# Modulation vectors on VectorE, norms read from PSUM, split weights at block 2's entry: one change to a two-block transformer kernel

## The chip, the cores and the metric

The kernel runs on one core of one Trainium2 chip. The metric is the device time of one execution in microseconds, and lower is better. A core has five engines that matter here: TensorE (PE, matmuls), VectorE (DVE), ScalarE (ACT), GpSimd (POOL) and SyncE (SP), which issues most transfers. Each engine takes its instructions in the order of its own queue, and semaphores order the engines among each other. SBUF is the memory on the chip, PSUM the eight banks (2 KB a partition each) into which TensorE writes.

## What is computed

256 tokens of width 1024 go through two blocks. The first is a mixer of three branches, a cross attention and 32 experts; the second has two layers, each with a mixer, a feed-forward part, and modulation by vectors that come from a condition `c`. Cut to what matters here:

```python
a = a_in[..., :D] * sigmoid(a_in[..., D:])
a = silu(layer_norm(causal_depthwise_conv(a, conv_a_w) + conv_a_b))
y_a = a @ w_a_out + b_a_out
y_b = (gate_b * causal_depthwise_conv(gate_c * v_bc, conv_b_w)) @ w_b_out
y_c = einsum(multiscale_pool(pool_in), pool_w) * pool_scale    # windows 2, 4, 8, 16
m = sigmoid(g_a) * y_a + sigmoid(g_b) * y_b + sigmoid(g_c) * y_c
x = layer_norm(ALPHA * x + m @ w_mix_out)
x = layer_norm(ALPHA * x + cross_attention(x, layer_norm(mem)))
x = layer_norm(ALPHA * x + experts(x))                         # top 4 of 32
for layer in range(2):                                         # block 2
    shift_m, scale_m, gate_m, shift_f, scale_f, gate_f = split(silu(c) @ ada_w[layer] + ada_b[layer], 6)
    h = rms_norm(x) * (1 + scale_m) + shift_m
    x = x + gate_m * (attention(h) if layer == 0 else retention(h))
    h = rms_norm(x) * (1 + scale_f) + shift_f
    x = x + gate_f * swiglu(h)
```

All is in float32.

## The kernel before, in words

Activations lie with features on the 128 partitions, in eight chunks of 128 features by 256 tokens. A **product** (`product`, L407) makes two chunks of output from eight chunks of input: 48 matmuls of 128x256, three for each pair, since each operand is split in a high and a low half. The halves of a weight are made on the chip by `Weights.split` (L276 to L293): ScalarE copies the high half `wh` (L289), VectorE subtracts it for the low half `wl` (L290), two splits of 128x1024 a product. GpSimd does the subtraction where the running number of the split stands in `ASIDE`. Raw weights come in tiles of 2 MB from a ring of five (`RB`), which the modulation tiles `wadb` share; all these loads go out on SP's queue. Activations are split the same way by `split` (L475 on ScalarE, L476 on VectorE).

The program is one long sequence of products. Two hooks put other work among them: `spare[0]()` is called as each product starts, and `pump` runs queued background steps (the 31 taps of the convolution, the chunks of a norm) at points within it. A scheduler then orders each engine's queue, so the order of emission is what the code decides.

**Block 1** runs the products `a1`, `a2`, four of pooling, then twelve of the short convolution (`gate_c`, `v_bc`, `gate_b` for each of four groups `j`), `pool_w`, the gate of the third branch, eight of gate and `yb`, four of `ga`, four of keys, four of values, four of `ya`, four of the mixing output, then cross attention, router and experts. A pooling product's result is written by ScalarE to `up`, one part of the tile `pads` (L756); GpSimd forms the window sums from it in one to four steps (L762). All four groups use the same pads.

**Norms** are made by `Stat`: squares and sums per chunk, TensorE sums over features (`sums`, L495 being one of the matmuls of `spread`), `roots` forms mean and reciprocal root, and `spread` (L488 to L496) writes a vector of tokens across the partitions of a PSUM tile by two matmuls with a diagonal made on VectorE (L494) or ScalarE (L492). `normal` then does, per chunk, the addition of the mean (L571), the multiplication by gain and root (L574), and a split. The mean is copied from PSUM to SBUF (`tmp_mu`) by ScalarE ahead of L571, and every third L571 is on GpSimd.

**Modulation vectors**: `vector_ada` (L608 to L628) handles 24 tiles `wadb` of four blocks, 128x1024 each, 96 blocks in all. A block is multiplied by `silu(c)` spread over the partitions (`cb`) and summed. By `POOLED`, 60 blocks are multiplied on GpSimd (L621) and summed on ScalarE (L622); the other 36 are one instruction on VectorE (L624). L626 adds the bias after each fourth block. A tile's load is issued when its first block is due. In block 1, 24 blocks run from the value products on (`early`: two a product in the first four, then one); after the experts `later` runs as many as `DUE` says, one a product from the fourth call on. `silu_c` (L605) computes `silu(c)` on ScalarE, which needs another table of functions.

**Entry of block 2.** The last norm of block 1 and the first of block 2 are done at once: `scale3` spreads four vectors to PSUM (`nmc`, `rrc`, `rmc`, `rsc`), `h0` makes each chunk of the input for block 2 (L1288 add, L1290 ScalarE, L1291, L1293 add, then `split` to `HH`, `HL`), and `back` restores the chunk of the running sum. Four products run first on uncorrected input, and `fix3` corrects their results (L1271, L1273, L1275, and L1276 on GpSimd).

Of the kernel before, what the change touches and what calls it, by code (L numbers as in the profile page):

```python
# [11 lines left out]
F32 = mybir.dt.float32  # L12
# [17 lines left out]
F3 = 1  # L30
# [17 lines left out]
DUE = '0001111111111111111'  # L48
# [5 lines left out]
POOLED = (4, 2)  # L54
TWO = 4
UB3 = 4
K3 = 4
GA = (1, 3, 5, 7)
GB = ()
ASIDE = (3, 5, 7, 9)  # L60
# [49 lines left out]
def host_layout(inp):  # L110
# [204 lines left out]
def program(ctx: ExitStack, tc: tile.TileContext, A, out, stop=None):  # L315
# [182 lines left out]
    class Stat:  # L498
# [23 lines left out]
        def finish(self, eps):  # L522
            self.sums()
            self.roots(eps)
            return self.nm
# [13 lines left out]
        def roots(self, eps):  # L539
# [3 lines left out]
            if self.center:  # L543
# [12 lines left out]
            b = psum([128, T], tag="st", bufs=2)  # L556
# [6 lines left out]
    def normal(src, dst, H, L, c, nm, g, b, func=None):  # L563
# [32 lines left out]
    vec = [None, 0, 0]  # L596
    cbs = []
    where = [0]

    def silu_c(pool, after=None):  # L600
# [3 lines left out]
        with paced() if after is None else behind(after):  # L604
            i = S.activation(cb, cb, AF.Silu).ins  # L605
        cbs[:] = [cb]
        return i

    def vector_ada(n=1):

        for _ in range(n):
            if vec[0] is None:
                if not late:
                    return
                vec[:] = [B.raw.tile([128, 4, D], F32, tag="raw", name="wadb"), 0, late.popleft()]
                nc.sync.dma_start(vec[0], A["wadb"][vec[2]])
# [42 lines left out]
    def router_constants():  # L659
# [5 lines left out]
        G.memset(rwx[:, :, NE:], 1.0 / D)  # L665
        for k in range(NCH):
# [1247 lines left out]
```

## Time and profile before

| | |
|---|---|
| time of three runs, us | 2196.34, 2203.99, 2202.17; median 2202.17 |
| the profiled execution, us | 2199.12 |
| its span in the profile, us | 2197.2 |
| TensorE busy | 2090.4 us, 95% |
| VectorE, ScalarE, GpSimd busy | 53%, 36%, 24% |
| mean clock granted to TensorE | 0.975 of full speed |

The span runs from the first to the last instruction in the trace; the profiled execution's own time has 1.9 us around it. The busy shares are means over stages with different limits: the experts, from some 460 to 1400 us, wait for transfers, the rest is paced by TensorE and by what feeds it. The page is read for where to look, the table by stretch for which stretch loses time, and the waits and the groups of such a stretch for what it loses it to.

### The profile page before, as it was taken

The page shows a single profiled execution, that of the slowest core. Times are in us where ns is not written, and L with a number is a line of the kernel's source. Part 1 is how long each engine was busy: PE and PEld are TensorE (multiplying, and loading weights), DVE is VectorE, ACT ScalarE, POOL GpSimd, SP SyncE. Part 2 cuts the span into 40 slices and gives each one's busy share as a digit, 9 for nine tenths or more (in the row PEclk, how much of TensorE's full clock was granted, in tenths as well). Part 3 has the DMA queues.
Part 4 walks back from the last instruction along what each step waited for, and adds up shares of the span by engine and source line. Part 5 has one row for each costly group of instructions (what it writes and reads, how often), then busy time and mean ns, then how long its engine had stood idle before and what let it go on. Part 6 is the DMA issues. An engine that isn't in the chain of part 4 may idle for free.

```text
span 2197.2 us, 32992 instructions
## 1 busy us (share of the span) xinstructions
PE 2090.4 (95%) x13668; PEld 1522.4 (69%) x13668; DVE 1159.1 (53%) x1815; ACT 800.1 (36%) x1374; POOL 532.7 (24%) x444
## 2 busy tenths in 40 slices
PE   8999988999998999999999999979999999999998
PEld 8999988873443333333333333568899999999998
DVE  6798888832322222222211112388797678877553
ACT  5576665630000000000000000365575465546443
POOL 2648386412000000000000000176412123310000
PEclk9999989999999999999999999989999999999999
DMA  8445555689999999999999999844377567555440
GB/s 347 165 158 192 200 202 197 246 330 394 392 420 384 428 428 427 426 428 427 428 427 427 427 427 428 352 155 159 124 301 274 209 237 272 227 191 225 189 154 20
DMA packets 49595, 650.57 MB, mean 296 GB/s; under 512 B 5632, under 2 KB 7552, under 8 KB 10656
## 3 DMA queue, kind: packets, MB, share of 16 engines
q1 hardware_dynamic: 48096, 645.45, 72.2%
q10 hardware_dynamic: 1344, 2.95, 0.4%
q8 instruction: 109, 1.79, 0.3%
q14 instruction: 46, 0.38, 0.0%
HBM read 647.33 MB, written 1.05 MB: 295 GB/s over the span
## 4 chain that ended last, share of the span: by engine, by line
PE 51%; DMA 5%; DVE 5%; issue 3%; ACT 2%; POOL 1%; DVEq 0%; ACTq 0%; POOLq 0%
PE ps_mm L1720 9%; PE ps_mm L418 8%; PE ps_mm L420 8%; PE ps_mm L419 8%; PE ps_st L1883 7%; DMA wgu<-in_wgu 5%; PE ps_tp L1774 2%; PE ps_tp L1707 1%; PE ps_mm L443 1%; PE ps_mm L444 1%; DVE act L1760 1%; PE ps_mm L445 1%; DVE wl L290 1%; POOL tmp_pd L1759 1%; PE ps_mm L1636 1%
## 5 line engine op out<-in xcount | busy, mean ns | idle before, releaser
L290 DVE TENSOR_TENSOR wl<-wraw,wh 128x1024 fp32r<-128x1024 f32 x352 | 487.4, 1387 | 192.7 <-ACT wh L289 190.5
L289 ACT ACTIVATE wh<-wraw 128x1024 fp32r<-128x1024 f32 x356 | 375.3, 1056 | 266.7 <-PE ps_mm L419 238.4
L1720 PE MATMUL ps_mm<-wgu,xs 128*64 128x512 f32 x2048 | 454.6, 594 | 7.5 <-DMA wgu<-in_wgu 6.9
L1720 PEld LDWEIGHTS ps_mm<-wgu,xs 128*64 128x64 f32 x2048 | 145.6, 137 | 287.7 <-issue 270.9
L1883 PE MATMUL ps_st<-wdn,actT 128*64 128x512 f32 x1024 | 233.3, 602 | 5.6 <-DVE actT L1768 5.6
L418 PE MATMUL ps_mm<-HH,wh 128*128 128x256 f32 x832 | 235.8, 284 | 0.7 <-ACT wh L289 0.7
L420 PE MATMUL ps_mm<-HH,wl 128*128 128x256 f32 x832 | 234.4, 284 | 1.7 <-DVE wl L290 1.7
L419 PE MATMUL ps_mm<-HL,wh 128*128 128x256 f32 x832 | 235.7, 284 | 0.0
L1756 DVE TENSOR_SCALAR tmp_pd<-ps_mm 128x512 f32<-128x512 f32 x32 | 22.1, 692 | 381.7 <-PE ps_mm L1720 381.6
L1759 POOL TENSOR_TENSOR tmp_pd<-tmp_pd,tmp_stat 128x512 f32<-128x512 f32 x32 | 40.1, 1275 | 752.9 <-ACT tmp_stat L1757 752.9
L621 POOL TENSOR_TENSOR wadb<-wadb,cb 128x1024 f32<-128x1024 f32 x60 | 169.4, 2848 | 141.7 <-DMA wadb<-in_wadb 101.6
L418 PE MATMUL ps_mm<-pairA,wh 128*128 128x256 f32 x640 | 184.1, 290 | 12.6 <-ACT wh L289 7.8
L1757 ACT ACTIVATE tmp_stat<-tmp_pd 128x512 f32<-128x512 f32 x32 | 20.1, 631 | 469.1 <-DVE tmp_pd L1756 469.1
L419 PE MATMUL ps_mm<-pairA,wh 128*128 128x256 f32 x640 | 184.0, 288 | 1.9 <-DVE pairA L476 1.9
L420 PE MATMUL ps_mm<-pairA,wl 128*128 128x256 f32 x640 | 181.7, 287 | 1.3 <-DVE wl L290 1.3
L1883 PEld LDWEIGHTS ps_st<-wdn,actT 128*64 128x64 f32 x1024 | 73.8, 138 | 139.5 <-issue 129.1
L420 PEld LDWEIGHTS ps_mm<-HH,wl 128*128 128x128 f32 x832 | 158.7, 192 | 3.0 <-DVE wl L290 2.3
L418 PEld LDWEIGHTS ps_mm<-HH,wh 128*128 128x128 f32 x832 | 159.4, 192 | 1.8 <-ACT wh L289 1.2
L419 PEld LDWEIGHTS ps_mm<-HL,wh 128*128 128x128 f32 x832 | 159.6, 192 | 0.9 <-issue 0.7
L418 PEld LDWEIGHTS ps_mm<-pairA,wh 128*128 128x128 f32 x640 | 125.6, 197 | 13.8 <-ACT wh L289 7.8
L419 PEld LDWEIGHTS ps_mm<-pairA,wh 128*128 128x128 f32 x640 | 126.0, 197 | 2.3 <-DVE pairA L476 2.3
L420 PEld LDWEIGHTS ps_mm<-pairA,wl 128*128 128x128 f32 x640 | 124.8, 196 | 1.7 <-DVE wl L290 1.7
(460 smaller groups left out, 4176.3 us busy)
## 6 DMA issues: line engine op xcount, KB each, us to landing
wgu<-in_wgu SPq DMA_DIRECT2D x128, 2048.0 KB, 22.5
wdn<-in_wdn SPq DMA_DIRECT2D x62, 2048.0 KB, 19.8
wraw<-in_wpost SPq DMA_DIRECT2D x56, 2048.0 KB, 7.7
wraw<-in_wpre SPq DMA_DIRECT2D x32, 2048.0 KB, 7.8
wadb<-in_wadb SPq DMA_DIRECT2D x24, 2048.0 KB, 9.1
wdn<-in_wdn SPq DMA_DIRECT2D x8, 512.0 KB, 24.4
wraw<-in_wpre SPq DMA_DIRECT2D x4, 512.0 KB, 8.0
wraw<-in_wpost SPq DMA_DIRECT2D x4, 512.0 KB, 11.7
```

The lines of the kernel that those rows point to most:

```text
L289: self.ins = (nc.scalar.activation(wh, src, AF.Copy).ins, (eng or nc.vector).tensor_tensor(wl, src, wh.bitcast(F32), op=ALU.subtract).ins)
L290: (eng or nc.vector).tensor_tensor(wl, src, wh.bitcast(F32), op=ALU.subtract).ins)
L418: PE.matmul(pts[m], wh[:, w], XH[:, kc, :width], start=(i == 0), stop=False)
L419: PE.matmul(pts[m], wh[:, w], XL[:, kc, :width], start=False, stop=False)
L420: PE.matmul(pts[m], wl[:, w], XH[:, kc, :width], start=False, stop=(i == n - 1))
L443: PE.matmul(pts[t], XH[:, kc, x], wh, start=(i == 0), stop=False)
L621: G.tensor_tensor(w[:, i, :], w[:, i, :], cbs[0], op=ALU.mult)
L1720: i_ = PE.matmul(banks[j][row[x]], xs[:, k, row[x]], r["g", k][:, x, 512 * j:512 * j + 512], start=False, stop=(k == NCH - 1))
L1756: V.tensor_scalar(g, banks[h], 7.0, None, op0=ALU.min)
L1759: G.tensor_tensor(g, g, s, op=ALU.mult)
L1774: PE.matmul(p[:, m, :], Y[:, (2 * c + m) * 128:(2 * c + m) * 128 + 128], GST, start=True, stop=True)
L1883: PE.matmul(yb[j][row[x]], actT[:, k, row[x]], r["d", j, k // 4][:, k % 4, x, :], start=(k == 0), stop=(k == NCH - 1))
```

## The change

1. **Modulation vectors.** All 96 blocks run as one VectorE instruction each. A tile's load is issued when the third block of the tile before has been emitted (`ada_load`, `coming`). The 24 blocks of block 1 start at the gate and `yb` products, and `EARLY` says how many each product gets: one in each of gate, `yb` and `ga`, none with keys and values, two with `ya`, one with the mixing output. After the experts `DUE` gives none in the first six calls and two in calls 17 to 19. `silu_c` runs ahead of the gate products; block 2's SiLU moves from the entry to the call with number 5.
2. **Norms.** With `bank=True` (memory norm, convolution norm, the rms norms of block 2) the mean's spread is made by ScalarE and stays in PSUM, in one bank with the root's; all L571 are on VectorE, and intermediate results lie in PSUM too.
3. **Entry of block 2.** The four spread vectors lie in two banks, `h0` is all VectorE with `nmc` and `w` in PSUM, `fix3` uses GpSimd every other time, and ten splits in place of four have their low half made on GpSimd.
4. **Pooling** product `j` is followed by the three products `j` of the short convolution.
5. **Router constants** (16 small GpSimd operations, two sums on TensorE) are made step by step over the first three `ya` products.

```diff
-F3 = 1
-DUE = '0001111111111111111'
+DUE = '0000001111111111222'
-POOLED = (4, 2)
-TWO = 4
+LEFT = (18, 0)
+EARLY = '11111111' + '1111' + '0000' + '0000' + '2222' + '1111' + '0000' + '0000'
-GA = (1, 3, 5, 7)
-GB = ()
-ASIDE = (3, 5, 7, 9)
+ASIDE = (2, 3, 4, 5, 6, 7, 8, 9, 10, 11)
+SILU = 5
...
     for j in range(4):
-        sl += wi("pool", j)
-    for j in range(4):
-        sl += wi("gc", j) + wi("v", j) + wi("gb", j)
+        sl += wi("pool", j) + wi("gc", j) + wi("v", j) + wi("gb", j)
...
-                b = psum([128, T], tag="st", bufs=2)
-                spread(b, nm, V)
-                mu = tmp(tag="mu", bufs=1)
-                S.activation(mu, b, AF.Copy)
+                if bank:
+                    both = psum([128, 2, T], tag="st", bufs=2)
+                    mu = both[:, 0]
+                    spread(mu, nm, S)
+                else:
...
-            b = psum([128, T], tag="st", bufs=2)
+            b = both[:, 1] if bank else psum([128, T], tag="st", bufs=2)
             i_ = spread(b, rs, S)
...
-            E = G if c % 3 == 2 else V
+            E = G if c % 3 == 2 and not bank else V
             E.tensor_tensor(x, x, mu, op=ALU.add)
-        t = tmp(tag="n", bufs=NB)
+        t = psum([128, T], tag="tp", bufs=2) if bank and mu is None else tmp(tag="n", bufs=NB)
...
-            y = tmp(tag="n", bufs=NB)
+            y = psum([128, T], tag="tp", bufs=2)
             S.activation(y, t, func, bias=b)
...
+    def ada_load():
+        if len(late) > LEFT[where[0]]:
+            w, g = B.raw.tile([128, 4, D], F32, tag="raw", name="wadb"), late.popleft()
+            nc.sync.dma_start(w, A["wadb"][g])
+            coming.append((w, g))
...
             with paced():
-                if i < POOLED[where[0]]:
-                    G.tensor_tensor(w[:, i, :], w[:, i, :], cbs[0], op=ALU.mult)
-                    S.activation(w[:, i, :], w[:, i, :], AF.Copy, accum_out=ADA[:, k:k + 1])
-                else:
-                    V.tensor_tensor_reduce(w[:, i, :], w[:, i, :], cbs[0], 1.0, 0.0, op0=ALU.mult, op1=ALU.add, accum_out=ADA[:, k:k + 1])
+                V.tensor_tensor_reduce(w[:, i, :], w[:, i, :], cbs[0], 1.0, 0.0, op0=ALU.mult, op1=ALU.add, accum_out=ADA[:, k:k + 1])
...
             vec[1] += 1
+            if i == 2:
+                ada_load()
...
+        silu_c(pre)
+        early_due = deque(int(x) for x in EARLY)
+
+        def early():
+            vector_ada(early_due.popleft())
+
+        ada_load()
+        spare[0] = early
...
-        nmc, rrc, rmc, rsc = (psum([128, T], tag=t, bufs=2) for t in ("tp", "st", "st", "tp"))
+        nmc, rrc, rmc, rsc = (b[:, i] for b in (psum([128, 2, T], tag="st", bufs=2) for _ in range(2)) for i in range(2))
...
-            if F3:
+            n3[0] += 1
+            if n3[0] % 2:
                 i = V.tensor_tensor(t, t, rrc, op=ALU.mult).ins
...
-                E = G if c in GA else V
-                E.tensor_tensor(a, a, nmb, op=ALU.add)
-                w, v = (tmp(tag="n", bufs=NB) for _ in range(2))
+                V.tensor_tensor(a, a, nmc, op=ALU.add)
+                if c % 2 == 0:
+                    pairs[0] = psum([128, 2, T], tag="tp", bufs=2)
+                w, v = pairs[0][:, c % 2], tmp(tag="n", bufs=NB)
...
-                E = G if c in GB else V
-                E.tensor_tensor(v, v, w, op=ALU.add)
-                split(HH[:, c, :], HL[:, c, :], v)
+                V.tensor_tensor(w, v, w, op=ALU.add)
+                split(HH[:, c, :], HL[:, c, :], w)
...
         def later():
+            if calls[0] == SILU:
+                with paced():
+                    i = S.activation(cbp, cbp, AF.Silu).ins
+                cbs[:] = [cbp]
+                with tc.issue_after(i):
+                    S.preload_act_table_set("natural_log_exp_and_others")
+                ada_load()
+            calls[0] += 1
             vector_ada(due.popleft() if due else 1)
...
-        if FIRST:
-            silu_c(post, root)
-        else:
-            with tc.issue_after(silu_c(post, root)):
-                S.preload_act_table_set("natural_log_exp_and_others")
```

## Rows read from the trace of the kernel before

**Rows 1.** the page, engines: busy us (share of the span) and instructions

```profile
PE 2090.4 (95%) x13668; PEld 1522.4 (69%) x13668; DVE 1159.1 (53%) x1815; ACT 800.1 (36%) x1374; POOL 532.7 (24%) x444
```

**Rows 2.** the table by stretch: length, engines' busy us, clock, DMA share, GB/s

```profile
76.00:100.00 24.00, 19.98 (x153) 19.57 (x152) 16.85 (x23) 12.87 (x22) 21.59 (x20) 0.93 0.47 176
100.00:188.00 88.00, 86.28 (x717) 85.81 (x716) 83.91 (x135) 62.84 (x109) 47.86 (x46) 1.00 0.42 156
188.00:234.00 46.00, 46.00 (x386) 46.00 (x385) 39.54 (x60) 28.72 (x48) 32.07 (x31) 1.00 0.49 184
234.00:282.00 48.00, 48.00 (x405) 48.00 (x405) 38.98 (x64) 36.41 (x60) 18.57 (x17) 1.00 0.58 220
282.00:326.00 44.00, 34.81 (x239) 34.13 (x238) 35.31 (x34) 27.28 (x50) 42.47 (x30) 0.81 0.52 195
326.00:348.00 22.00, 18.79 (x130) 18.27 (x129) 15.88 (x19) 11.47 (x22) 12.14 (x5) 0.84 0.25 96
348.00:410.00 62.00, 56.94 (x436) 55.76 (x436) 58.63 (x71) 38.40 (x70) 46.22 (x30) 0.92 0.57 216
...
460.00:1400.00 940.00, 903.13 (x4335) 369.93 (x4334) 208.30 (x395) 70.34 (x149) 62.51 (x76) 0.99 0.99 417
...
1426.00:1480.00 54.00, 40.65 (x282) 37.38 (x280) 42.93 (x64) 32.17 (x60) 37.53 (x27) 0.84 0.40 154
...
1592.00:1630.00 38.00, 36.85 (x303) 36.19 (x302) 35.26 (x68) 30.12 (x53) 5.82 (x2) 1.00 0.75 300
...
1799.00:1814.00 15.00, 12.78 (x95) 12.57 (x94) 14.94 (x25) 9.50 (x18) 7.08 (x4) 0.89 0.61 235
```

**Rows 3.** waits of TensorE, 76 to 100 us: us in total, times, longest

```profile
PE ps_mm L418 <- ACT pads L756: 4.0, 2, 3.2
```

**Rows 4.** waits of TensorE, 282 to 326 us

```profile
PE ps_st L495 <- DVE tmp_t L494: 5.7, 2, 4.3
PE ps_mm L444 <- DVE wl L290: 3.4, 1, 3.4
```

**Rows 5.** VectorE's groups, 282 to 326 us: busy us, mean ns | idle before

```profile
L571 DVE TENSOR_TENSOR cvap<-cvap,tmp_mu 128x256 f32<-128x256 f32 x6 | 7.6, 1332 | 0.0
...
L574 DVE SCALAR_TENSOR_TENSOR tmp_n<-cvap,cols,ps_st 128x256 f32<-128x256 f32 x4 | 1.9, 469 | 0.0
```

**Rows 6.** instructions of line 571: ns minimum/median/maximum, first and last start

```profile
L571 DVE TENSOR_TENSOR MT<-MT,tmp_mu x6: 411/412/961, 242.1 to 244.9; 128x256 f32<-128x256 f32 x6
```

**Rows 7.** waits of TensorE, 1426 to 1480 us

```profile
PE ps_mm L445 <- DVE HL L476: 8.8, 5, 3.8
```

**Rows 8.** VectorE's groups, 1426 to 1480 us

```profile
L476 DVE TENSOR_TENSOR HL<-tmp_n,HH 128x256 fp32r<-128x256 f32 x8 | 8.3, 1032 | 0.0
...
L1273 DVE TENSOR_TENSOR tmp_t<-tmp_t,ps_st 128x256 f32<-128x256 f32 x8 | 3.2, 415 | 0.1
```

**Rows 9.** instructions of line 621, and what GpSimd idled for before them

```profile
L621 POOL TENSOR_TENSOR wadb<-wadb,cb x60: 2340/2606/3427, 278.7 to 1932.6; 128x1024 f32<-128x1024 f32 x60
...
  DMA wadb<-in_wadb: 101.6, 11
```

**Rows 10.** instructions of line 624

```profile
L624 DVE CUSTOM_DVE_ANT_0 wadb<-wadb,cb x36: 1208/1218/3439, 1470.6 to 1973.4; 128x1024 f32<-128x1024 f32 x36
```

**Rows 11.** ScalarE's groups, 1420 to 1480 us

```profile
L1290 ACT ACTIVATE tmp_n<-ps_st,ADA,k 128x256 f32<-128x256 f32 x8 | 4.4, 560 | 6.5 <-DVE HL L476 6.5
...
L605 ACT ACT_TABLE_LOAD x1 | 1.3, 1283 | 0.0
...
L605 ACT ACTIVATE cb<-cb 128x1024 f32<-128x1024 f32 x1 | 1.1, 1057 | 0.0
```

**Rows 12.** waits of VectorE, 1424 to 1480 us

```profile
DVE tmp_t L1271 <- ACT tmp_mu L1260: 5.0, 1, 5.0
```

**Rows 13.** instructions of line 290, on VectorE and on GpSimd

```profile
L290 DVE TENSOR_TENSOR wl<-wraw,wh x352: 1202/1225/3435, 7.8 to 2177.7; 128x1024 fp32r<-128x1024 f32 x176
...
L290 POOL TENSOR_TENSOR wl<-wraw,wh x4: 2401/2498/2565, 1410.9 to 1446.0; 128x1024 fp32r<-128x1024 f32 x4
```

More of the change, by code (lines that the diff above doesn't have):

```diff
@@ L520, in add, with finish @@
                 G.tensor_tensor(sq, sq, q, op=ALU.add)
-        def finish(self, eps):
+        def finish(self, eps, bank=False):
             self.sums()
-            self.roots(eps)
+            self.roots(eps, bank)
             return self.nm
@@ L537, in sums, with roots @@
             return i_.ins
-        def roots(self, eps):
+        def roots(self, eps, bank=False):
             e = self.e
@@ L548, in roots @@
                 S.activation(rs, rs, AF.Sqrt, bias=eps)
-                b = psum([128, T], tag="st", bufs=2)
-                spread(b, nm, V)
-                mu = tmp(tag="mu", bufs=1)
-                S.activation(mu, b, AF.Copy)
+                if bank:
[3 more added lines that the diff above has]
+                else:
+                    b = psum([128, T], tag="st", bufs=2)
+                    spread(b, nm, V)
+                    mu = tmp(tag="mu", bufs=1)
+                    S.activation(mu, b, AF.Copy)
             else:
@@ L561, in program, with normal @@
     line = []
-    def normal(src, dst, H, L, c, nm, g, b, func=None):
+    def normal(src, dst, H, L, c, nm, g, b, func=None, bank=False):
         mu, rs = nm
@@ L596, in program, with silu_c @@
     vec = [None, 0, 0]
+    coming = deque()
     cbs = []
     where = [0]
-    def silu_c(pool, after=None):
+    def silu_c(pool):
         cb = pool.tile([128, D], F32, tag="cb", name="cb")
         nc.sync.dma_start(cb, A["cb"])
-        with paced() if after is None else behind(after):
-            i = S.activation(cb, cb, AF.Silu).ins
+        with paced():
+            S.activation(cb, cb, AF.Silu)
         cbs[:] = [cb]
-        return i
+    def ada_load():
[3 more added lines that the diff above has]
+            coming.append((w, g))
     def vector_ada(n=1):
@@ L612, in vector_ada @@
             if vec[0] is None:
-                if not late:
+                if not coming:
+                    ada_load()
+                if not coming:
                     return
-                vec[:] = [B.raw.tile([128, 4, D], F32, tag="raw", name="wadb"), 0, late.popleft()]
-                nc.sync.dma_start(vec[0], A["wadb"][vec[2]])
+                vec[:] = [coming[0][0], 0, coming.popleft()[1]]
             w, i, g = vec
@@ L665, in router_constants @@
         G.memset(rwx[:, :, NE:], 1.0 / D)
+        yield
         for k in range(NCH):
@@ L675, in router_constants @@
         V.tensor_copy(rc[:, 0], p[:, 0])
+        yield
     mid = ctx.enter_context(ExitStack())
@@ L753, in program, with pooling, pool_in @@
             G.memset(t[:, :, 0:16], 0.0)
-        for j in range(4):
-            def pool_in(m, p, j=j):
+        def pooling(j):
+            def pool_in(m, p):
                 S.activation(up[:, m, 16:], p, AF.Identity, bias=col("b_in", 40 + 2 * j + m))
@@ L776, in program, with gated @@
             G.memset(t[:, 0:2], 0.0)
-        for j in range(4):
+        def gated(j):
             gcs = []
@@ L803, in program @@
             product(wst, XH, XL, R8, gate_b, taps=TAPS[2])
+        for j in range(4):
+            pooling(j)
+            gated(j)
         M = single()
@@ L840, in program @@
             product(wst, YH, YL, R8, yb, taps=TAPS[6])
-        nm = st.finish(eps5)
+        nm = st.finish(eps5, True)
         MH, ML = pair("C", F32R)
         for c in range(NCH):
-            normal(MT, None, MH, ML, c, nm, col("mem_ln_g", c), col("mem_ln_b", c))
+            normal(MT, None, MH, ML, c, nm, col("mem_ln_g", c), col("mem_ln_b", c), bank=True)
         SG, KT = pair("D")
@@ L896, in program @@
             product(wst, AH, AL, R8, ya)
+            if j < 3:
+                next(routing)
         if stop == "m":
@@ L1099, in program @@
     spare[0] = lambda: None
-    while vec[0]:
-        vector_ada()
+    assert not vec[0] and not coming
     with tc.tile_pool(name="moe", bufs=1, reuse_waits="tile") as mo:
@@ L1168, in chain @@
                 for c in range(NCH):
-                    bg.append(lambda c=c: normal(X0, None, HH, HL, c, (None, rb), gain_[:, n, c:c + 1], mod[:, l, 3 * i, c:c + 1]))
+                    bg.append(lambda c=c: normal(X0, None, HH, HL, c, (None, st.nm[1]), gain_[:, n, c:c + 1], mod[:, l, 3 * i, c:c + 1], bank=True))
             def roots_then():
@@ L1265, in scale3 @@
             return i
+        n3 = [0]
         def fix3(p, y=None):
@@ L1318, in program @@
         due = deque(int(x) for x in DUE)
+        cbp = post.tile([128, D], F32, name="cbp")
+        nc.sync.dma_start(cbp, A["cb"])
+        calls = [0]
         def later():
+            if calls[0] == SILU:
+                with paced():
+                    i = S.activation(cbp, cbp, AF.Silu).ins
+                cbs[:] = [cbp]
+                with tc.issue_after(i):
+                    S.preload_act_table_set("natural_log_exp_and_others")
+                ada_load()
+            calls[0] += 1
             vector_ada(due.popleft() if due else 1)
```

14 lines of the change are left out of this document (5 added, 9 removed).

## The prediction, made before the changed kernel ran

> **What bounds the kernel now.** I read the page's engine table first: TensorE is busy 95% of the 2197.2 us span [rows 1], so only the few stretches in which it idles can give anything. The table by stretch shows them [rows 2]. From 188 to 234 us TensorE never stops and does 386 matmuls in 46.00 us, 119.2 ns each, so a product of 48 needs 5.72 us. Length less matmuls x 119.2 ns is then what a stretch loses: 76 to 100 us: 24.0 - 153 x 0.1192 = 5.8; 282 to 326: 44.0 - 28.5 = 15.5; 326 to 348: 22.0 - 15.5 = 6.5; 348 to 410: 62.0 - 52.0 = 10.0; 1426 to 1480: 54.0 - 33.6 = 20.4 (too high by a little, some matmuls there are small); 1799 to 1814: 15.0 - 11.3 = 3.7. In the experts, 460 to 1400 us, the DMA share is 0.99 and the change touches nothing. Whatever the work before the experts gains should pass through, since that DMA work can only start when its buffers are freed.
>
> The waits of TensorE name the cause in each. At 76 to 100 us it waits 4.0 us for ScalarE's write of `pads` (L756) [rows 3], which in turn waits for GpSimd's chain of window sums over the same pad; four pooling products in a row ask GpSimd for more than four products' time. At 282 to 326 us it waits 5.7 us for VectorE's L494 and 3.4 us for a weight split [rows 4]. Why VectorE is late there is in its groups of that stretch [rows 5]: L571, all operands in SBUF, takes 1332 ns in the mean, while L574, with one operand in PSUM, takes 469 ns in the very same stretch. On another tile, with GpSimd less busy, L571's median is 412 ns [rows 6]. So VectorE operations with two SBUF inputs wait for long GpSimd operations to end, and those with a PSUM input don't. GpSimd is busy 42.47 of the 44 us [rows 2]. The same picture stands at block 2's entry: TensorE waits 8.8 us for L476 [rows 7], and there L476 takes 1032 ns in the mean, beside 415 ns for L1273 with an operand in PSUM [rows 8].
>
> [...]
>
> **The change part by part.**
>
> **Modulation vectors.** GpSimd loses 60 multiplies of 2.606 us in the median [rows 9], about 156 us of its time; VectorE gains 60 blocks at 1.22 us [rows 10], say 1.3 with the short instruction that reads each sum out,, 24 of them in block 1 and 36 after the experts. ScalarE loses its 60 sums. What goes: in 282 to 326 us twelve of those multiplies, that is most of GpSimd's load, and the 16 small router operations that are now spread over the `ya` products. With them goes the contention of [rows 5]. The norm of the convolution's output has four value products (22.9 us) to hide under and its operations at their lone prices fit. I take 13.5 of the 15.5 us lost, with 8 to 15.5 as bounds; late next is the statistics' own chain, which I leave 2 us.
>
> What comes: the 24 blocks of block 1 now lie on VectorE. In the eight gate and `yb` products (188 to 234 us) VectorE is busy 39.54 of 46 us [rows 2]; eight blocks make it 39.5 + 10.4 = 49.9, 3.9 us over TensorE's time. Its splits are waited for by TensorE within a product or two, so I count -5 (bounds -8 and 0, the latter if background convolution taps slide into the key products, which get no block). `ga`, four blocks with 38.98 of 48 busy around it: -1. `ya` has two blocks a product, 10.4 us in four products: VectorE's 15.88 us of 326 to 348, some of it contention, would come to 24 to 26 against 22.9; the 6.5 lost there fall to some 3.5: +3 (bounds -3 and +6). From 348 to 410 us VectorE is busy 58.63 of 62 us and GpSimd 46.22; GpSimd's modulation blocks leave, VectorE gets four (5.2 us), for which the contention hides room: +2 (bounds -5 and +7).
>
> After the experts the pace stays about one block a product. In the long stretches VectorE has room for 0.65 us more a product, but around 1571 to 1630 us it hasn't: three calls with two blocks each catch up there, and VectorE is busy 35.26 of 38 us from 1592 [rows 2]. The extra blocks on VectorE, four or five at 1.30 = 5 to 6 us, have some 2 us of room: -4 (bounds -7 and 0). The 3.7 us lost at 1799 to 1814, a weight split late beside GpSimd's multiply: +3 (0 to +3.7).
>
> The loads now go out when the third block of the tile before is done. GpSimd waited 101.6 us for 11 of them [rows 9], 9.2 us each, at no cost on that engine. On VectorE such a wait would hold up the weight splits queued behind it. With one block a product the lead is two products, 11.4 us, enough for 9.2; with two it is one, 5.7. I cost it at nothing for the first case; the second is in the bounds and in a rival.
>
> **SiLU.** Block 1's moves from the front of the value products to the gate products; the table load of 1.28 us and the 1.06 us of work [rows 11] lie beside TensorE's full stretch: -1 with its table switch back. Block 2's went out at its entry, and with a table load on either side it held ScalarE about 3.6 us; VectorE waited 5.0 us for ScalarE's L1260 then [rows 12]. That goes, and comes back at call 5 amid running products: -1.5 there.
>
> **Entry of block 2.** Per chunk VectorE does four operations: before, the add (half of them), L1291, the second add L1293 and L476 at 1032 ns; now all four have a PSUM operand, three at 415 ns as L1273 and one at 469 as L574 [rows 5, 8], 1.71 us, 13.7 us for eight. The removal of ScalarE's 3.6 us and of VectorE's weight splits, ten of which GpSimd takes, comes on top. Against it: a split takes GpSimd 2498 ns against 1225 on VectorE [rows 13], so two a product are 5.0 of 5.72 us, and GpSimd has its multiplies L1299 and half of the `fix3` adds besides. TensorE's need is 8 chunks in 5.72 us, so some 6 to 8 us stay lost: of 20.4 I take 13 (bounds 4 and 18).
>
> Operands in PSUM have the same price by the rows: L1273 415 ns with one, L571 412 ns without [rows 6, 8]. [...]
>
> **Pooling alternates.** A pooling product now has three gated ones behind it, 22.9 us for GpSimd's sums, where 24 us held 21.59 us of its work [rows 2], so the wait for `pads` goes: +5 of 5.8 (bounds 2 and 5.8; late next are VectorE's taps, 83.91 of 88 us from 100 us on [rows 2]).
>
> GpSimd's FIFO in the attention (1480 to 1571 us), free of the multiplies, gives +2 (0 to +3).
>
> **Sum.** Block 1: 13.5 - 5 - 1 + 3 + 2 - 1 + 5 = 16.5. Block 2: 13 - 4 + 3 - 1.5 + 2 = 12.5. Together 29. The profiled execution took 2199.1 us, so 2170.1; it stands 3 us under the median of the three runs and inside their spread of 7.7 us, so I don't correct for that.
>
> **The rivals.**
>
> *VectorE becomes the bound in block 1's middle.* All 24 blocks there fall on an engine at 80 to 95%. For it: 83.91 of 88 and 58.63 of 62 us. Against: the contention leaves with GpSimd's multiplies. Price: the longest block took 3439 ns [rows 10]; if one in four of the 24 meets a GpSimd operation like that, 6 x 2.2 = 13 us: 2183.
>
> *VectorE waits for the loads (the other side).* If the prefetch comes late, because the weights hold the ring's five buffers or because landing takes the 9.2 us and the lead is one product, each of 24 tiles stalls VectorE, first in its queue, by 9.2 - 5.7 = 3.5 us: 84 us, so 2254. It decides from 29 / 24 = 1.2 us a tile on. For it: the 101.6 us. Against: most calls carry one block.
>
> *The entry doesn't do what it says.* GpSimd, with 37.53 of 54 us busy [rows 2] and six more splits (15 us) less some 14 us of multiplies and adds, is as full as before, and its splits hold up VectorE's remaining ones. ScalarE and VectorE also share the bank of each pair: if they take turns, 8 x 0.56 us (L1290) [rows 11] = 4.5 us is added. Then the entry gains 4, not 13: 2179. [...]
>
> **How the numbers follow.** A measurement here tells some 0.3%, 6.6 us, from no change: faster is under 2195.6, slower over 2208.8. Forecast 0.64, own range 2150 to 2190; VectorE bound 0.17, 2170 to 2205; loads 0.11, 2200 to 2255; entry 0.08, 2170 to 2190. Faster: 0.62 + 0.13 + 0.07 = 0.82; same 0.06; slower 0.12. The bounds of the parts, not all at once at one end, give 2142 at the low side; at the high one 2197 takes in VectorE's case and leaves out the loads.
>
> **What would show it.** Right: TensorE's waits for L494, L476 and `pads` gone, L571 and L476 at 410 to 480 ns throughout, the clock near 0.95 at 282 to 326 us, VectorE near full from 188 to 234. Wrong: waits of VectorE for `wadb` loads, TensorE waiting for `wl` in the gate or `ya` products, GpSimd's `wl` as the releaser at the entry.

## The result, and the profile of the changed kernel

The changed kernel takes 2165.4 us (2160.6 to 2167.1, four runs) beside 2200.8 us before: a ratio of 0.9837, with a 95% interval of 0.9812 to 0.9862. That is 35.4 us less, where the prediction had 2170.1 and 29 us. Its profiled execution took 2160.6 us with a span of 2158.8; it is the fastest of the four.

The table by stretch of the changed kernel, at the places that answer to those of [rows 2] (length; busy us and instructions of TensorE, its weight loads, VectorE, ScalarE, GpSimd; clock, DMA share, GB/s):

```profile
74.00:92.00 18.00, 18.00 (x152) 18.00 (x151) 17.93 (x30) 11.33 (x21) 9.49 (x8) 1.00 0.48 175
92.00:186.00 94.00, 90.33 (x740) 90.13 (x739) 84.12 (x129) 69.17 (x115) 60.34 (x59) 0.98 0.42 158
186.00:230.00 44.00, 42.10 (x334) 41.31 (x333) 42.74 (x66) 24.51 (x43) 35.91 (x29) 0.96 0.60 231
...
276.00:312.00 36.00, 36.00 (x305) 36.00 (x304) 28.65 (x47) 24.18 (x43) 5.96 (x5) 1.00 0.45 170
312.00:332.00 20.00, 17.75 (x134) 17.34 (x133) 18.72 (x38) 10.31 (x18) 6.68 (x6) 0.91 0.70 267
332.00:392.00 60.00, 56.95 (x422) 56.31 (x420) 45.74 (x80) 28.37 (x49) 31.48 (x34) 0.89 0.53 205
...
1400.00:1443.00 43.00, 37.93 (x286) 36.32 (x286) 27.04 (x65) 32.46 (x58) 25.68 (x20) 0.96 0.49 191
...
1536.00:1560.00 24.00, 17.16 (x122) 16.31 (x121) 19.91 (x40) 13.60 (x27) 1.67 (x3) 0.79 0.53 202
...
1762.00:1775.00 13.00, 12.11 (x101) 11.90 (x100) 13.00 (x27) 6.25 (x10) 1.82 (x2) 1.00 0.60 233
```

With the prediction's measure (length less matmuls x 0.1192 us), the value products lose nothing (36.0 - 36.4) where they lost 15.5, at a clock of 1.00 in place of 0.81 and with GpSimd at 5.96 us in place of 42.47; block 2's entry loses 43.0 - 34.1 = 8.9 in place of 20.4. The gate and `yb` products now lose 44.0 - 39.8 = 4.2, and 332 to 392 us, which now holds the sums of the router constants, loses 9.7.

The new losses have names. Waits of TensorE in the changed kernel, from four stretches (140 to 165, 332 to 392, 1400 to 1443 and 1536 to 1560 us; total us, times, longest):

```profile
PE ps_mm L414 <- ACT z L824: 3.7, 1, 3.7
...
PE ps_tp L681 <- POOL rwx L676: 3.1, 3, 1.9
...
PE ps_mm L414 <- ACT VT L1417: 3.7, 1, 3.7
...
PE ps_st L491 <- ACT tmp_t L488: 4.1, 1, 4.1
```

The first is the `pool_w` product behind the last short convolution. The second is the router constants: their matmuls stand in TensorE's queue ahead of the last `ya` product and wait for GpSimd. The third is the SiLU, which ScalarE does just then (first of the two timelines below). The fourth is the entry of the first feed-forward part: VectorE does four modulation blocks in a row (second timeline) ahead of the reciprocal L557, on which L488 and L491 hang.

GpSimd's operations that the second loss waits for (ns minimum/median/maximum):

```profile
L676 POOL TENSOR_SCALAR rwx<-tmp_t,cols x8: 358/884/2402, 328.6 to 337.2; 128x32 f32<-128x32 f32 x8
```

In the kernel before the same eight took 360/469/1513 ns. The two longest here, 2402 and 2380 ns, each overlap two VectorE operations of 128x1024 in a row: two modulation blocks in the one case, a split and a block in the other. So GpSimd also waits for VectorE, and the blocks that went to VectorE are part of it. ScalarE's and VectorE's timelines for the third and the fourth loss:

```profile
1429.01 1.28 ACT L1350 ACT_TABLE_LOAD   x1
1430.31 1.06 ACT L1350 ACTIVATE cbp<-cbp 128x1024 f32<-128x1024 f32 x1
1431.38 1.28 ACT L1353 ACT_TABLE_LOAD   x1
...
1435.23 0.63 ACT L1417 ACTIVATE VT<-ps_mm 128x256 f32<-128x256 f32 x2
```

```profile
1539.59 1.21 DVE L630 CUSTOM_DVE_ANT_0 wadb<-wadb,cbp 128x1024 f32<-128x1024 f32 x1
...
1543.02 1.22 DVE L630 CUSTOM_DVE_ANT_0 wadb<-wadb,cbp 128x1024 f32<-128x1024 f32 x1
...
1544.96 0.15 DVE L557 RECIPROCAL tmp_rs<-tmp_rs 128x2 f32<-128x2 f32 x1
```

Every kernel here runs the same 13668 matmuls, and, but for the pooling and for small ones that the scheduler moves, in the same sequence. So the traces can be laid side by side by the rank of the matmul, at ranks where each kernel has done the same work but for at most 12 matmuls. The table gives the us between matmuls of these ranks in each profiled execution; the runs are told of below. "Gate/yb" includes the start of `ga`, "values" the rest of `ga`, the keys and the values; "mix" is half of the mixing output, and "cross" begins with the other half.

```
from rank        0     624    1440   1920   2415   2648   2736   3408   7824   8064   8400   9024
to rank         624    1440   1920   2415   2648   2736   3408   7824   8064   8400   9024  10464
               pool   to gate gate/yb values  ya     mix   cross experts entry  att.   ffn0   ffn0
before         84.3  101.8   57.3   75.0   34.6   14.7   97.7  951.9   47.5   49.5   87.3  175.6
changed        79.4  103.3   61.7   59.1   38.3   10.6   91.8  948.8   36.6   44.2   93.2  173.6
pooling alone  79.7  104.7   58.8   75.3   31.2   15.6   97.0  948.2   46.3   42.8   88.5  176.9
norms alone    83.8  101.8   57.3   66.7   32.9   14.3   97.8  952.1   46.0   42.9   93.3  176.6
vectors alone  83.3  103.2   61.7   60.6   37.0   11.7   90.1  951.1   41.1   43.1   93.4  174.0
entry alone    82.9  102.8   58.8   75.0   32.4   13.4   98.2  952.9   47.9   52.5   94.1  177.5
 once more     84.3  101.8   57.3   75.0   33.0   13.4   98.2  955.0   44.4   53.3   95.6  176.9
entry, 4       83.0  102.9   58.8   75.0   32.4   13.4   98.3  954.9   41.2   44.6   96.7  175.7
eight memsets  83.4  101.8   58.8   75.1   30.6   15.6   97.0  948.1   46.3   42.7   94.6  176.9
no entry part  79.5  103.5   61.7   59.1   38.3   10.6   91.8  948.7   41.3   42.9   98.1  173.6
late loads     78.7  105.4   61.8   59.1   38.4   10.6   90.3  951.2   36.7   45.3   94.0  172.9
four mended    78.9  103.4   58.8   60.6   35.4   10.5  100.0  948.6   33.9   43.7  101.4  173.7
two mended     79.8  103.4   61.6   60.7   40.7   10.6   92.4  948.1   33.9   43.1   98.6  173.8
```

"Entry alone" and "once more" are two executions of one program: a single trace is good to some 2 us in the experts and 3.5 at the entry.

### The profile page after: what moved, and what is told of

Read it like the earlier page. It is cut to its first block, busy times and chain, and to the rows that moved or that the text cites. A ratio compares the mean times of both kernels' runs of the same rounds, so it can differ in the third digit from the quotient of the medians.

```text
span 2158.8 us, 32876 instructions
## 1 busy us (share of the span) xinstructions
PE 2075.2 (96%) x13668; PEld 1513.4 (70%) x13668; DVE 1117.9 (52%) x1937; ACT 739.6 (34%) x1257; POOL 368.4 (17%) x378
## 4 chain that ended last, share of the span: by engine, by line
PE 54%; DVE 5%; DMA 3%; issue 3%; ACT 2%; POOL 1%; DVEq 0%; ACTq 0%; POOLq 0%
PE ps_mm L1750 11%; PE ps_mm L414 9%; PE ps_mm L415 8%; PE ps_mm L416 8%; PE ps_st L1913 8%; DMA wgu<-in_wgu 3%; PE ps_tp L1804 2%; PE ps_tp L1737 2%; DVE act L1790 1%; PE ps_mm L439 1%; PE ps_mm L440 1%; PE ps_mm L441 1%; POOL tmp_pd L1789 1%; PE ps_mm L1666 1%; DVE wl L286 1%
## 5 line engine op out<-in xcount | busy, mean ns | idle before, releaser
L286 DVE TENSOR_TENSOR wl<-wraw,wh 128x1024 fp32r<-128x1024 f32 x346 | 435.8, 1261 | 190.1 <-ACT wh L285 188.9
L1919 ACT ACTIVATE Y<-ps_st 128x256 f32<-128x256 f32 x32 | 12.2, 383 | 288.2 <-PE ps_st L1913 279.3
```

What stands on the lines that cost most here:

```text
L286: (eng or nc.vector).tensor_tensor(wl, src, wh.bitcast(F32), op=ALU.subtract).ins)
```

## The experiments

**One part at a time, on the kernel before.** The first, pooling alone:

```diff
-        sl += wi("pool", j)
-    for j in range(4):
-        sl += wi("gc", j) + wi("v", j) + wi("gb", j)
+        sl += wi("pool", j) + wi("gc", j) + wi("v", j) + wi("gb", j)
```

> The kernel before with only the order of pooling and short convolution changed. Theory: GpSimd's window sums over the one set of pads were what TensorE waited for at 76 to 100 us; with three products between two pooling products the 4.0 us wait for pads is gone, the stretch up to the pool_w products is 5 to 7 us shorter, and nothing later changes: 2194 to 2197 us against 2200.8. Rival: the same GpSimd and VectorE work only comes due later, the pool_w products wait for the last group's split instead, and 3 to 5 us are given back there: 2198 to 2201 us.

Measured: 2192.1 us, ratio 0.9966 (0.9948 to 0.9983). The pooling stretch gains 4.6 us, and 2.9 are given back by rank 1440, as the rival had it: in a `pool_w` product TensorE waits for VectorE's part of the last short convolution (140 to 196 us).

```profile
PE ps_mm L416 <- DVE tmp_t L799: 5.1, 1, 5.1
```

Most of the gain in time lies where the pooling isn't: 6.7 us in the attention. Both theories missed that.

The norms alone (the edits of `finish`, `roots`, `normal` and its callers):

```diff
-        nm = cst_.finish(eps5)
+        nm = cst_.finish(eps5, True)
-            E = G if c % 3 == 2 else V
+            E = G if c % 3 == 2 and not bank else V
```

> The kernel before with only the norms' operands in PSUM; GpSimd still does its twelve multiplies of the modulation beside the convolution's norm. Theory (VectorE operations with two SBUF inputs wait for long GpSimd operations, those with a PSUM input don't): L571's operation takes 410 to 420 ns in that stretch although GpSimd is as busy as before (some 42 of 44 us), and of the 15.5 us lost there 8 to 10 come back; the time is 2188 to 2193 us. Rival (GpSimd's multiplies delay VectorE in some other way, by its queue or the weight splits alone): the operation still takes 1000 ns or more in the mean and the time is 2198 to 2202 us.

Measured: 2187.0 us, ratio 0.9936 (0.9916 to 0.9956). VectorE's groups from 276 to 318 us in this run, and the stretch itself:

```profile
L290 DVE TENSOR_TENSOR wl<-wraw,wh 128x1024 fp32r<-128x1024 f32 x11 | 24.9, 2267 | 3.8 <-ACT wh L289 3.8
...
L578 DVE TENSOR_TENSOR cvap<-cvap,ps_st 128x256 f32<-128x256 f32 x3 | 1.2, 407 | 0.0
```

```profile
276.00:318.00 42.00, 38.46 (x288) 37.43 (x287) 36.97 (x32) 30.79 (x54) 40.25 (x19) 0.92 0.56 218
```

GpSimd is busy 40.25 of 42 us with its multiplies, the splits still take 2267 ns, and the addition of the mean, now with one operand in PSUM, takes 407 ns where it took 1332 [rows 5]. The stretch up to the end of the values falls by 8.3 us. The theory holds; the norm's operands alone are some half of the 15.9 us that all parts bring there.

The modulation vectors alone (`vector_ada`, `ada_load`, `EARLY`, `DUE`, both SiLUs):

```diff
-                if i < POOLED[where[0]]:
-                    G.tensor_tensor(w[:, i, :], w[:, i, :], cbs[0], op=ALU.mult)
-                    S.activation(w[:, i, :], w[:, i, :], AF.Copy, accum_out=ADA[:, k:k + 1])
-                else:
-                    V.tensor_tensor_reduce(...)
+                V.tensor_tensor_reduce(...)
```

> The kernel before with only the modulation vectors changed: all on VectorE, spread anew, SiLU moved in both blocks. Theory: L571 with its operands still in SBUF takes some 412 ns beside the values, since GpSimd's long multiplies are gone; 10 to 13 us come back there, 4 are lost in the gate and yb products where VectorE is the bound, the entry of block 2 gains about 4 without the SiLU and loses 4 where the SiLU went, 2.5 are lost at the first feed-forward part: 2188 to 2193 us. Rival: VectorE becomes the bound in block 1 and eats the gain, 2198 to 2205 us.

Measured: 2173.6 us, ratio 0.9875 (0.9847 to 0.9903), 14 us below the theory's range. The stretch up to the end of the values falls by 14.4 us, nearly as much as with all parts together (15.9), and that with all operands in SBUF:

```profile
L572 DVE TENSOR_TENSOR cvap<-cvap,tmp_mu 128x256 f32<-128x256 f32 x6 | 3.2, 598 | 0.0
```

The gate and `yb` products lose 4.4 us (4 were expected), the entry gains 6.4 (4 were expected), and the theory had nothing for 7.6 us in the cross attention. GpSimd's work there no longer stands behind multiplies; that this is the reason is not shown. `ya` loses 2.4 us, and TensorE waits there for the router constants (285 to 356 us), which this run makes where the kernel before makes them:

```profile
PE ps_tp L677 <- POOL rwx L673: 2.9, 2, 1.8
```

The entry of block 2 alone, ten splits on GpSimd:

```diff
-GA = (1, 3, 5, 7)
-GB = ()
-ASIDE = (3, 5, 7, 9)
+ASIDE = (2, 3, 4, 5, 6, 7, 8, 9, 10, 11)
...
-                E.tensor_tensor(a, a, nmb, op=ALU.add)
-                w, v = (tmp(tag="n", bufs=NB) for _ in range(2))
+                V.tensor_tensor(a, a, nmc, op=ALU.add)
+                if c % 2 == 0:
+                    pairs[0] = psum([128, 2, T], tag="tp", bufs=2)
```

> The kernel before with only the entry of block 2 changed (operands in PSUM, shared banks, ten splits on GpSimd); the SiLU stays at the entry. Theory: the split of HL and the adds take 410 to 480 ns in place of 1000, and this by itself brings 9 to 12 of the entry's 20 us: 2189 to 2192 us. Rival: what held the entry was ScalarE with the SiLU and its table loads, so the entry alone brings 3 to 4 us: 2197 to 2198 us.

Measured: 2208.2 us, ratio 1.0031 (1.0015 to 1.0047): slower, against both. Waits of TensorE from 1428 to 1540 us, then VectorE's and GpSimd's timelines:

```profile
PE ps_mm L417 <- DVE wl L287: 7.5, 1, 7.5
PE ps_tp L1401 <- DVE az L1408: 7.3, 1, 7.3
```

```profile
1452.92 10.96 DVE L621 CUSTOM_DVE_ANT_0 wadb<-wadb,cb 128x1024 f32<-128x1024 f32 x1
1463.82 0.07 DVE L621 DVE_READ_ACCUMULATOR2_ANT ADA<- 128x1 f32 x1
1463.82 2.35 DVE L287 TENSOR_TENSOR wl<-wraw,wh 128x1024 fp32r<-128x1024 f32 x2
```

```profile
1452.29 4.79 POOL L618 TENSOR_TENSOR wadb<-wadb,cb 128x1024 f32<-128x1024 f32 x2
1456.98 0.79 POOL L1276 TENSOR_TENSOR tmp_t<-tmp_t 128x256 f32<-128x256 f32 x1
1457.68 1.46 POOL L1302 TENSOR_TENSOR X<-X,tmp_sq 128x256 f32<-128x256 f32 x2
1459.05 2.40 POOL L287 TENSOR_TENSOR wl<-wraw,wh 128x1024 fp32r<-128x1024 f32 x1
1461.35 0.77 POOL L1302 TENSOR_TENSOR X<-X,tmp_sq 128x256 f32<-128x256 f32 x1
1462.04 0.77 POOL L1276 TENSOR_TENSOR tmp_t<-tmp_t 128x256 f32<-128x256 f32 x1
```

One VectorE block of 1.2 us lasts 10.96 us: it starts 0.6 us into the first of eight GpSimd operations, and its own 1.2 us end 1.0 us after the last of them. Its tile had landed at 1445.1 us, so it wasn't waiting for data. The weight split that TensorE needs stands behind it in VectorE's queue.

**Is it the splits?** The same kernel with four splits on GpSimd:

```diff
-ASIDE = (2, 3, 4, 5, 6, 7, 8, 9, 10, 11)
+ASIDE = (3, 5, 7, 9)
```

> The run with block 2's entry alone (2208 us), but with four weight splits on GpSimd, as before, in place of ten. Theory: what made that run slower was GpSimd's unbroken run of splits, multiplies and adds, against which one VectorE block with two SBUF inputs took 10.97 us and TensorE waited 7.5 us for the split behind it; with six splits fewer no VectorE instruction takes over 4 us and the time is 2190 to 2198 us. Rival: the shared banks and PSUM operands cost it, so it stays at 2203 to 2209.

Measured: 2193.5 us, ratio 0.9968 (0.9950 to 0.9986), 14.7 us less. VectorE's blocks (ns minimum/median/maximum):

```profile
L621 DVE CUSTOM_DVE_ANT_0 wadb<-wadb,cb x36: 1210/1219/3425, 1458.5 to 1972.8; 128x1024 f32<-128x1024 f32 x36
```

The entry falls from 47.9 to 41.2 us with the same shared banks and PSUM operands, and the attention from 52.5 to 44.6. So the six splits more on GpSimd made the loss, and the rival falls. By what way is shown for the entry, by the block. In the attention TensorE waits 7.3 us for L1408 with ten splits and not with four, but there the queues of VectorE and GpSimd are also in another order, so this half may be the order's.

The ten-split kernel once more, unchanged, for its trace:

> The run with block 2's entry alone, once more, for its trace. If VectorE's 10.97 us block is what GpSimd's unbroken run of eight operations does to it, the same block takes 10 to 11 us again beside the same eight operations, and TensorE waits 7 to 8 us for the split behind it. If it was a chance of one execution, the block takes 1.2 to 3.6 us, TensorE's wait is gone, and the time is 7 us shorter, 2198 to 2202 us.

```profile
L621 DVE CUSTOM_DVE_ANT_0 wadb<-wadb,cb x36: 1209/1218/10399, 1452.9 to 1985.1; 128x1024 f32<-128x1024 f32 x36
```

```profile
PE ps_mm L417 <- DVE wl L287: 7.5, 1, 7.5
PE ps_tp L1401 <- DVE az L1408: 7.4, 1, 7.4
```

Minimum, median and maximum of the 36 blocks, and TensorE's waits: the block takes 10.40 us beside the same eight operations, and TensorE's two waits are the same. The block is no chance; the time was 2211.6 us.

**How long does VectorE wait for GpSimd?** Behind the last output, GpSimd gets runs of multiplies and VectorE one instruction beside each:

```diff
+            for q in range(n):
+                G.tensor_tensor(wide4[:, 1, :size], wide4[:, 0, :size], wide4[:, 2, :size], op=ALU.mult)
...
+                V.tensor_tensor_reduce(wide4[:, 3, :], wide4[:, 0, :], wide4[:, 0, :], 1.0, 0.0, op0=ALU.mult, op1=ALU.add, accum_out=ADA[:, 0:1])
```

> The changed kernel with a measurement behind its last output, so only the tail of the trace counts: GpSimd gets unbroken runs of 8 multiplies of 128x1024 or 12 of 128x256, all from and to SBUF, and as each run begins VectorE gets one instruction: a multiply of 128x1024 with two SBUF inputs, the same with a sum (the form of the modulation blocks), or a multiply of 128x256 with one PSUM input. Theory A: a VectorE instruction with two SBUF inputs waits for the one GpSimd operation under way: some 3.5 us beside the long ones and 2 us beside the short ones, whichever the form. Theory B: it waits until GpSimd leaves a gap, so 15 to 20 us and 8 to 10 us. Theory C: the plain multiply waits for one operation and the form with a sum for the whole run. The one with a PSUM input takes 410 to 420 ns by all three.

VectorE's timeline at the run of short multiplies:

```profile
2174.72 0.42 DVE L1630 TENSOR_TENSOR tmp_t<-tmp_n,ps_mm 128x256 f32<-128x256 f32 x1 [7.40 <-POOL tmp_n L1620]
2175.06 1.39 DVE L1634 CUSTOM_DVE_ANT_0 bench<-bench 128x1024 f32<-128x1024 f32 x1
```

The block with a sum took 1.39 us and the one with a PSUM input 0.42, by theory A. But the scheduler pulled the long runs forward beside weight splits (one took 2.59 us), and beside the block with a sum GpSimd did three short multiplies, 3.19 us in all. So it shows waits of at most one operation there, and says nothing on a run of eight.

**Does the order alone move the time?** Pooling alone and norms alone both gained in the attention, which neither touches. Laid side by side, the built programs differ there: the scheduler orders each queue by a timeline of its own, so an edit in block 1 shifts it and reorders block 2. The test is an edit with no purpose:

```diff
             G.memset(t[:, :, 0:16], 0.0)
+            V.memset(tmp((128, T)), 0.0)
...
```

(eight in a row after each of three pads, 24 in all).

> The kernel before with eight VectorE memsets of an unused 128x256 tile put in front of the pooling; nothing else. They cost 1 to 3 us of VectorE, but the scheduler now orders VectorE's and GpSimd's queues after the experts exactly as in the run with the pooling order alone. Theory: the 9 us that that run gained at the entry and in the attention came from this order, not from the pooling; they appear here too, entry and attention take 75 to 77 us in place of 85.3, and the time is 2191 to 2196 us. Rival: they came with the pooling in another way (an earlier start, other transfers), so this run takes 2200 to 2204.

Measured: 2192.4 us, ratio 0.9969 (0.9949 to 0.9989). The idle work makes the kernel 8.5 us faster. The attention takes 42.7 us and entry and attention together 89.0 in place of 97.0 (the expectation's 85.3 has other limits), with work that is the same. After the experts VectorE's and GpSimd's orders are those of the run with the pooling alone, instruction for instruction, and so is the time to 0.3 us. So of the pooling's own gain nothing is left that a measurement can tell. By the table the eight memsets' gain is 3.1 us at the ranks 2415 to 2736 and 3.8 in the experts, which vary from 948.1 to 954.9 us among the runs here; the 8.0 gained at entry and attention are given back by 7.3 at the feed-forward part.

**The changed kernel without the entry's part:**

```diff
-ASIDE = (2, 3, 4, 5, 6, 7, 8, 9, 10, 11)
+ASIDE = (3, 5, 7, 9)
...
-                V.tensor_tensor(a, a, nmc, op=ALU.add)
+                E.tensor_tensor(a, a, nmb, op=ALU.add)
```

> The changed kernel with block 2's entry as it was before (four splits on GpSimd, adds of alternate chunks on GpSimd, operands in SBUF, four banks); the other four parts as changed. Theory now: with GpSimd free of multiplies and the SiLU gone, the entry's own part is worth only the difference between the stretch of entry and attention in the run with the vectors alone (72.8 us) and in the changed kernel (69.3): 2168 to 2171 us. The prediction's view, that the PSUM operands and the splits carry most of 13 us, expects 2174 to 2178. A rival: the entry's part costs here as it did alone, 2155 to 2160.

Measured: 2166.7 us, ratio 0.9848 (0.9817 to 0.9878). In the traces the entry takes 41.3 us without it and 36.6 with it, and the first feed-forward part 98.1 and 93.2; in the time it is 1.3 us, inside the interval. So the time doesn't show what the entry's part adds to the other four. None of the three expectations is right.

**Loads late:**

```diff
-            if i == 2:
-                ada_load()
...
-        ada_load()
...
-                ada_load()
```

> The changed kernel with each modulation tile's load issued only when its first block is due, as before, in place of the early issue. Theory of the prediction's rival: VectorE, first in its queue, then waits for the landings, 7.6 us each less the 2 to 4 us of slack it has, at most of the 24 tiles: 50 to 100 us more, 2215 to 2265. Other theory: the scheduler places the block where it expects the data, weights behind it are two products ahead, and only a few tiles hurt: 2166 to 2180.

Measured: 2164.6 us, ratio 0.9843 (0.9814 to 0.9872), no difference. VectorE idled before no block for a landing. So the early issue isn't needed.

**Mending the new losses.** Four at once:

```diff
-EARLY = '11111111' + '1111' + '0000' + '0000' + '2222' + '1111' + '0000' + '0000'
+EARLY = '00000000' + '1111' + '0000' + '0000' + '1111' + '2222' + '1111' + '1111'
-DUE = '0000001111111111222'
+DUE = '0000001111112222211'
...
+        nc.sync.dma_start(scratch, cb)
...
-            if j < 3:
+            if j < 2:
                 next(routing)
...
-        nc.sync.dma_start(cbp, A["cb"])
+        nc.sync.dma_start(cbp, scratch)
```

> The changed kernel with four of its own new losses taken away: the early blocks leave the gate and yb products (none there, one each with ga, ya, the query and output products, two with the mixing output); the router constants' matmuls are emitted after the second product of the mixing output, not between the third and fourth ya product; after the experts the calls with two blocks are 13 to 17, in the attention, not 17 to 19; silu(c) of block 1 is kept in device memory and read back, so block 2 does no SiLU, only the table load at the same call. Theory: the steps of 4.2 us (gate and yb), 5.5 us (router constants), 4.9 us (SiLU) and 2.4 us (first feed-forward part) go, some 12 to 15 us: 2150 to 2154 us. Rival: the scheduler's new order gives as much back as it takes: 2160 to 2167.

Measured: 2169.0 us, ratio 0.9867 (0.9846 to 0.9888). The gate and `yb` products take 58.8 us (-2.9), `ya` 35.4 (-2.9) and the entry 33.9 (-2.7), each less than the 4.2, 5.5 and 4.9 expected; the router's matmuls still wait for L678 (3.6 us), since the scheduler set them back to where they were. And 1.5 us come up at the values, 8.2 in the cross attention, where the query and output products now have blocks, and 8.2 at the feed-forward part. With two mended:

```diff
-EARLY = '11111111' + '1111' + '0000' + '0000' + '2222' + '1111' + '0000' + '0000'
+EARLY = '101010101111111100001111222200000000'
...
+        nc.sync.dma_start(scratch, cb)
...
-        nc.sync.dma_start(cbp, A["cb"])
+        nc.sync.dma_start(cbp, scratch)
```

> The changed kernel with two of its losses taken away, since the run with four of them showed which cost elsewhere: every other gate or yb product has a block, the four taken out go to the key products, ya has one a product and the mixing output two; silu(c) is kept in device memory, with the table load at the same call; calls after the experts and router constants as in the changed kernel. Theory: 2 to 3 us back in the gate and yb products, 3 with ya, 2 lost with the mixing output, 2.7 back at block 2's entry: 2158 to 2161 us. Rival: the key products (VectorE busy 41.8 of 46 us there) lose what the gate products gain, and the new order costs some us: 2164 to 2168.

Measured: 2165.5 us, ratio 0.9837 (0.9812 to 0.9862): the rival. The entry gives 2.7; gate and `yb` with the start of `ga` give only 0.1; the values take 1.6, `ya` 2.4 and the feed-forward part 5.4. No version tried beats the changed kernel.

## Why the prediction was right, and where not

The forecast of 29 us came from twelve terms, and the total came out at 35.4. By the table, whose profiled executions lie 38.5 us apart:

- **Values and the convolution's norm: 13.5 taken, 15.9 measured** up to rank 2415, the end of the values. The cause was as stated [rows 4, 5], and the signs that it named are there: L574 at 414 ns with all additions on VectorE, the clock at 1.00. What the sum didn't see is that two of the five parts cure the same stall: the norms alone give 8.3, the vectors alone 14.4, both 15.9.
- **`ya`: +3 taken, -3.7 measured.** This is the step that failed. The prediction looked for VectorE alone to be late there and gave the router constants no price. In the changed kernel TensorE waits 3.1 us for them, on top of 2.3 for the norm's chunks and a split, for which it waited 3.2 before. Their move alone is not the reason: the vectors alone, with the constants where they were, show 2.9 us of the same wait and 37.0 us for `ya`. With the values 14 to 16 us shorter TensorE comes to these sums earlier, and GpSimd makes the constants beside VectorE's blocks. No run took the wait away, so what it costs in time is not shown.
- **Mixing output and cross attention: +2 taken, 10.0 measured** (4.1 and 5.9), undersized: the vectors alone give 3.0 and 7.6.
- **Gate and `yb`: -5 taken, and -1 each for `ga` and block 1's SiLU; -4.4 measured**, from VectorE at 42.74 of 44 us. The rival of VectorE as the bound shows here and, with the four blocks in a row, at the first feed-forward part.
- **Pooling: +5 taken, 3.4 measured** in the trace (4.9 less 1.5 given back by rank 1440). The wait for `pads` is gone. Late next was not only VectorE, as the prediction had it: alone it is VectorE's short convolution (5.1 us), in the changed kernel it is ScalarE, 3.7 us late in emptying the PSUM tiles of the `pool_w` products (L824). In the time, the pooling alone can't be told from the run with eight memsets; what it adds to the other parts was not measured.
- **Entry: 13 taken, 10.9 measured.** The vectors alone reach 6.4 of it, the entry's part with four splits 6.3, so most of it does not hang on both. The prediction put ten splits on GpSimd down as help. Beside GpSimd's multiplies six of them cost 14.7 us of time, 6.7 of it at the entry; with the multiplies gone the entry has no such loss. The prediction did not price this dependence.
- **SiLU -1.5 and first feed-forward part -4 taken.** Without the SiLU the entry takes 33.9 us in place of 36.6 in both mended runs, so it costs some 2.7. From rank 8400 to 9024 the stretch is 5.9 longer; the blocks ahead of L557 explain a wait of 4.1, but the run with eight memsets, which moves no vectors, shows 7.3 there. How much is the blocks' and how much the order's stays open.
- **Attention: +2 taken, 5.3 measured**; the run with eight memsets gives 6.8. So GpSimd's freed queue, the prediction's reason, is not needed for it, and the 5.9 after it take it back.
- **Retention's entry: +3 taken, 0 net.** The stretch of 1762 to 1775 us loses 13.0 - 12.0 = 1.0 in place of 3.7, but the products right behind give it back: from rank 10464 to 10752 both kernels take 38.8 us.
- **Experts: nothing taken, 3.1 measured**, inside what they vary among the runs.
- **Loads at no cost:** right, and more than needed.
- **Operands in PSUM at no extra price:** right. In the changed kernel the addition of the mean takes 414 ns (L574), with a PSUM operand, and 412 before [rows 6]:

```profile
L574 DVE TENSOR_TENSOR cvap<-cvap,ps_st 128x256 f32<-128x256 f32 x8 | 3.3, 414 | 0.2 <-PE ps_st L491 0.2
```

At the entry ScalarE and VectorE share the bank of each pair. That they take turns there, 4.5 us in the prediction's rival, is shown by no run, and none has the same operands in banks of their own. In the changed kernel ScalarE's eight instructions that write to these banks take 526 ns in the mean (L1314), where those that wrote to SBUF took 560 [rows 11], and VectorE's that write there take 425 (L1316).

The four single parts sum to -9.4, -14.5, -27.9 and +6.7 us, 45.1 together, where the whole, which has the router constants besides, is 35.4. The overlap of norms and vectors, 6.8 us at the values, is one reason. A draw of the scheduler's order, some 8 us that three of the four may include as the eight memsets do, is probably the other; that share is argued, not shown. The closeness of the prediction is thus in part luck: the values are sound, but `ya` came out 6.7 us worse than its term and the mixing output with the cross attention 8.0 better, and the 3 of the experts and the 5 of the attention are no more than other orders give. Its low bound of 2142 us is also no sum of its parts: with all of them at their best ends they give 55.5 us, so 2143.6.

## What to carry to other kernels

Where a build-time scheduler sets the queues' order, run one edit that does nothing before a gain under half a per cent is put down to its reason. Two cures for one stall don't add, so price the second with the first already in. When a stall goes, ask what TensorE's queue then comes to sooner, and who makes it. Work handed to GpSimd is not free while its queue is full (six splits cost 14.7 us here): look at what else runs there in the same microseconds, and give VectorE's operations of that stretch an operand in PSUM (407 ns here in place of 1332).

## What was not expected of the hardware

A VectorE instruction with two SBUF inputs normally waited for one GpSimd operation. In the kernel before, 72 VectorE instructions took over 0.6 us more than the shortest of their form, 2.24 us at most. None of them has an operand in PSUM (those that do took at most 0.14 us more), and each ended within its own shortest time after the end of one GpSimd operation. In 40 of them the next GpSimd operation had begun by then without a gap, so VectorE did get in between, and a GpSimd operation that follows without a gap is not enough for a longer loss. The block at block 2's entry took 10.96 and 10.40 us beside eight in a row, in both executions. What singles this block out stays open; the measurement behind the last output says nothing on it.
